# Multi-query attention on one core: every engine's order taken from a virtual-time plan, 231 units of the exponential on VectorE, the last product of each wholly on GpSimd

## The chip, the cores and the metric

The kernel runs on one core of a Trainium2 chip. The metric is device time in microseconds, the median of several runs. The engines are TensorE (PE in the profile; its weight loads are PEld), VectorE (DVE), ScalarE (ACT) and GpSimd (POOL). SyncE (SP) only issues transfers here. PSUM takes the matmul results; SBUF holds everything else.

## The reference, cut to what matters

Eight batches, 1,024 positions, 16 query heads of 64 columns, and one key and one value head per batch that all query heads share.

```python
def reference(q, k, v):              # q 8x1024x16x64, k and v 8x1024x64
    q = q.transpose(0, 2, 1, 3)
    scores = np.matmul(q, k.transpose(0, 1, 3, 2)) / np.sqrt(head_dim)
    weights = np.exp(scores - np.max(scores, axis=-1, keepdims=True))
    weights = weights / np.sum(weights, axis=-1, keepdims=True)
    return np.matmul(weights, v).transpose(0, 2, 1, 3)
```

## The kernel before

**Units.** The work is cut into 1,024 units (STEPS, numbered u). A unit belongs to a pair of heads p, to one half c of the 1,024 queries and to one block j of 128 keys; eight units (NKT) with the same p and c are a set. Two score matmuls (L261), one per head and each on half of the array's rows, write a 128x1024 tile of scores in PSUM. There are three such tiles (scp), so three units can be between their score matmuls and the reading of their scores. No maximum is subtracted; a check of the sums at the end (L377 on) sets a flag, and another path runs if it is bad.

**The exponential, two ways.** Most units go to ScalarE: one ACTIVATE (L274) makes a 128x1024 weight tile "wt". Every fifth unit from step 10 to step 1000, 200 in all, goes to VectorE (`vector_exp`, L210), in five steps:

- bits (L215): scores in PSUM to 16-bit integers in SBUF, a half-precision number whose exponent is roughly right;
- mantissa (L221) and power (L231): the fraction and the exponent cut out of these bits, SBUF to SBUF;
- square (L242): the mantissa times itself, SBUF to SBUF;
- product: bits times square. GpSimd makes columns 512 to 1023 (L243), VectorE columns 0 to 511 (L249). VE_U = 512 is the point of division.

Such a unit has three weight tiles: power, bits and product, which are multiplied by value tiles scaled by C0, 1 and C3. Its values therefore take three matmuls where a ScalarE unit takes one.

**Values.** For each set there are eight outputs (four blocks of 128 queries, two heads), numbered gg over the whole kernel. Each is a chain of 128x65 matmuls (L335) over the eight units' weight tiles, 8 plus 2 for every VectorE unit in the set; column 65 holds the sum. Seven outputs (GB) share one PSUM bank; there are two banks. When a bank is full, VectorE takes the reciprocal of its sums (`inverse`, L277) and multiplies (`finish`, L286) into an output tile "osb" of 56 groups, one of two, from which SP's queue stores 8 groups at a time (L314). The last set has its own loop (L365).

**What sets the order.** Each engine runs its instructions in the order in which the program issues them. That order is dealt out by hand. `step` (L402) issues the score matmuls and the exponential of one unit and then up to two of VectorE's waiting steps from the list `pend`. `plan` (L412) says after which units values are issued, and how many: DEAL = (1, 1, 0, 1, 0), so after three of each five units. TensorE therefore turns from values to scores and back three times in five units. Evictions enter `pend` ahead of the other steps. VectorE's half of the product is issued right after the bits of the next VectorE unit.

**The rest.** `after` (L434) prefetches the next batch: GpSimd issues the loads of q (L125) and of v (L108), SP the turning of q (L135), GpSimd scales the keys in two instructions (`prep_k`, L194) and VectorE scales the values (`prep_v`, L206). It is called for the units since the last values, behind those values.

Of the kernel before, what the change touches and what calls it, by code (L numbers as in the profile page):

```python
# [10 lines left out]
FP32 = mybir.dt.float32  # L11
# [13 lines left out]
DEAL = (1, 1, 0, 1, 0)  # L25
DEAL_AT = 1
VE_U = 512
VE_N = 1
VE_M = 5
# [3 lines left out]
def attention_main(ctx, tc, q, k, v, out, flag):  # L33
# [11 lines left out]
    nc = tc.nc  # L45
# [11 lines left out]
    OCH = 7  # L57
# [8 lines left out]
    wtp = ctx.enter_context(tc.tile_pool(name="wtp", bufs=24))  # L66
    w3p = ctx.enter_context(tc.tile_pool(name="w3p", bufs=6))
    mp = ctx.enter_context(tc.tile_pool(name="mp", bufs=2))
    osbp = ctx.enter_context(tc.tile_pool(name="osbp", bufs=2))
# [11 lines left out]

    kv = {}
# [4 lines left out]
    ot = {}  # L87
    pend = []
    product = []
    late = []  # L90
# [48 lines left out]
    def bank(name):  # L139
        return op.tile([P, 512], FP32, tag="ot", name=name)  # L140
# [69 lines left out]
    def vector_exp(sc, p, c, j):  # L210
        w3 = w3p.tile([P, 3, 2, QCH], FP16, tag="w3", name=f"we{p}_{c}_{j}")
        m = mp.tile([P, 2, QCH], FP16, tag="m", name=f"m{p}_{c}_{j}")
        m2 = mp.tile([P, 2, QCH], FP16, tag="m2", name=f"mm{p}_{c}_{j}")
        t = w3[:, 1].bitcast(I16)
        nc.vector.tensor_scalar(  # L215
            out=t, in0=sc, scalar1=15.0 * 1024, scalar2=0.0, op0=ALU.add, op1=ALU.max
        )
        if product:
            pend.append(product.pop())
        pend.append(  # L220
            lambda: nc.vector.tensor_scalar(  # L221
                out=m.bitcast(I16),
                in0=t,
                scalar1=0x3FF,
                scalar2=0x3C00,
                op0=ALU.bitwise_and,
                op1=ALU.bitwise_or,
            )
        )
        pend.append(  # L230
            lambda: nc.vector.tensor_scalar(  # L231
                out=w3[:, 0].bitcast(I16),
                in0=t,
                scalar1=0x7C00,
                scalar2=None,
                op0=ALU.bitwise_and,
            )
        )
        we, wu, mm = (x.rearrange("p h q -> p (h q)") for x in (w3[:, 1], w3[:, 2], m2))

        def square():
            nc.vector.tensor_tensor(out=m2, in0=m, in1=m, op=ALU.mult)  # L242
            nc.gpsimd.tensor_tensor(  # L243
                out=wu[:, VE_U:], in0=we[:, VE_U:], in1=mm[:, VE_U:], op=ALU.mult
            )

        pend.append(square)
        product.append(
            lambda: nc.vector.tensor_tensor(  # L249
                out=wu[:, :VE_U], in0=we[:, :VE_U], in1=mm[:, :VE_U], op=ALU.mult  # L250
            )
        )
        wt[(p, c, j)] = [(w3[:, 0], 1), (w3[:, 1], 0), (w3[:, 2], 2)]

    def scores(p, c, j, by_vector):
        b = p // HP
        sc = scp.tile([P, 2, QCH], FP32, tag="sc", name=f"sc{p}_{c}_{j}")
        k2t = kv[b]["k2t"]
        for hh in range(2):
            r = 64 * hh  # L260
            nc.tensor.matmul(  # L261
                sc[:, hh, :],
                k2t[r : r + 64, j * P : (j + 1) * P],
                qt[b][r : r + 64, p % HP, c * QCH : (c + 1) * QCH],
                start=True,
                stop=True,
                tile_position=(r, 0),
            )
        if by_vector:
            vector_exp(sc, p, c, j)  # L270
            return
        w = wtp.tile([P, 2, QCH], FP16, tag="wt", name=f"wt{p}_{c}_{j}")
        wt[(p, c, j)] = [(w, 0)]
        nc.scalar.activation(out=w, in_=sc, func=EXP, scale=escale, bias=math.log(CS))  # L274

    def inverse(o, g0, n):
        nc.vector.reciprocal(out=rec_all[:, g0 : g0 + n], in_=o[:, 0:n, D])  # L277

    def finish(o, g0, n):

        rec = rec_all[:, g0 : g0 + n]
        i0 = g0 % (OCH * GRP)
        if i0 == 0:
            osb[0] = osbp.tile([P, OCH * GRP, D], FP32, tag="osb", name=f"osb{g0}")
# [23 lines left out]
    def store(ob, g0, g1):  # L308
# [3 lines left out]
        j0 = g0 % (OCH * GRP)  # L312
# [8 lines left out]
    def values(gg):  # L321


        p, c = divmod(gg // GRP, NCH)
        g = gg % GRP
        qb, hh = divmod(g, 2)
        if gg % GB == 0:
            ot[0] = bank(f"ot{gg}")[:, 0 : GB * 72].rearrange("p (g f) -> p g f", f=72)
        o = ot[0]
        vp = kv[p // HP]["vp"]  # L330
        terms = [(j, w, i) for j in range(NKT) for w, i in wt[(p, c, j)]]

        def one(n, j, w, i):
            last = n == len(terms) - 1
            nc.tensor.matmul(  # L335
                o[:, gg % GB, 0 : D + 1],
                w[:, hh, qb * P : (qb + 1) * P],
                vp[:, i, j, 0 : D + 1],
                start=(n == 0),
                stop=last,  # L340
            )
            if not last:
                return
            if gg % GB == GB - 1 or gg == NG - GRP - 1:
                late.append((o, gg - gg % GB, gg % GB + 1))
            if g == GRP - 1:
                for x in range(NKT):
                    del wt[(p, c, x)]

        return [lambda n=n, t=t: one(n, *t) for n, t in enumerate(terms)]  # L350

    def last_values():
# [8 lines left out]
        for j in range(NKT):  # L361
            ((w, i),) = wt[(p, c, j)]
# [10 lines left out]
        for h in range(2):  # L373
            inverse(os[h], NG - GRP + 4 * h, 4)
            finish(os[h], NG - GRP + 4 * h, 4)
# [17 lines left out]
    LAG = 2 * NKT + 2  # L393
    STEPS = NP * NCH * NKT
    PSTEPS = NCH * NKT
    LAST_VE = max(u for u in range(STEPS - 2 * NKT + 1) if u * VE_N % VE_M < VE_N)
    HURRY = STEPS - NKT - 6

    def to_vector(u):
        return NKT <= u <= LAST_VE and u * VE_N % VE_M < VE_N  # L400

    def step(u):  # L402
        p, r = divmod(u, PSTEPS)
        c, j = divmod(r, NKT)
        scores(p, c, j, to_vector(u))
        for _ in range(2):
            if pend:
                pend.pop(0)()
        if product and u >= LAST_VE + 2 and not pend:
            product.pop()()  # L410

    def plan():  # L412

        upto = [0]
        for g in range(STEPS):
            many = sum(to_vector(g // GRP * NKT + j) for j in range(NKT))
            upto.append(upto[-1] + NKT + 2 * many)
        due = {}  # L420
        for u in range(STEPS):
            if u >= HURRY:
                if u % 2:
                    due[u] = None
                continue
            n, i = divmod(u - DEAL_AT, len(DEAL))
            if DEAL[i]:
                at = DEAL_AT + len(DEAL) * (n + sum(DEAL[: i + 1]) / sum(DEAL)) - LAG
                at = max(at, 0.0)
                g = int(at)  # L430
                due[u] = round(upto[g] + (at - g) * (upto[g + 1] - upto[g]))
        return due
# [28 lines left out]
    with tc.manual_schedule():  # L461
# [28 lines left out]
        nxt = made = 0  # L490
        todo = []
        due = plan()
        us = []
        for u in range(STEPS):
            step(u)
            us.append(u)
            if u not in due:
                continue
            new = []
            for f in late:  # L500
                new += [lambda f=f: inverse(*f), lambda f=f: finish(*f)]
            if len(new) == 2:
                new[1:1] = pend[:1]
                del pend[:1]
            pend[:0] = new
            del late[:]
            if due[u] is not None:
                while made < due[u]:
                    if not todo:
                        todo = values(nxt)  # L510
                        nxt += 1
                    todo.pop(0)()
                    made += 1
            else:
                for _ in range(4):
                    if not todo and nxt < STEPS - GRP and nxt // GRP * NKT + NKT + 3 <= u:
                        todo = values(nxt)
                        nxt += 1
                    for f in todo:
                        f()  # L520
                    todo = []
            for x in us:
                after(x)
            us = []
        assert nxt == STEPS - GRP
        assert not product
        for f in pend:
            f()
        for f in late:
            inverse(*f)  # L530
            finish(*f)
# [128 lines left out]
```

## Time and profile before

The median of three runs is 774.12 us (773.71 to 774.24). The profiled execution is one of its own.

| What | Value |
|---|---|
| Span of the profiled execution | 771.9 us |
| Granted TensorE clock, mean | 0.995 |
| ScalarE's first exponential starts, last ends | 7.26 us, 765.9 us |
| VectorE's first bits (L215), last bits | 15.18 us, 748.58 us |
| Last GpSimd product (L243) ends | 752.70 us |
| Matmuls of the last set (L365) start | 763.90 us |
| Mean of one mantissa / power / square | 428 / 434 / 692 ns |
| Mean of one half product on VectorE / on GpSimd | 437 / 1154 ns |
| Mean of one inverse / one finish | 195 / 622 ns |
| Key scaling on GpSimd (L194) | 14 of 1652 ns |
| q loads issued by GpSimd (L125) | 64 of 604 ns |

Busy time is given per engine and per line of the program. In a group line, the shapes are those of output and input, then the number of instructions, the busy time of all of them in us, the mean of one in ns, and behind the bar the time for which the engine stood idle just before them, with what ended it. In a timeline line, the start in us comes first, then the time taken, engine, line, operation and tiles. VectorE's successive instructions overlap a little at their ends, so the distance from start to start is shorter than the duration.

### The profile page before, as it was taken

To read this page: it belongs to the slowest core of one execution; us is meant where nothing else is said; L and a number is where in the kernel's file an instruction comes from. 1 tells how busy PE (TensorE), PEld (TensorE's weight loads), DVE (VectorE), ACT (ScalarE), POOL (GpSimd) and SP (SyncE) were. 2 spreads that over 40 slices of the span, in tenths; PEclk is the share of its full clock that TensorE was granted. 3 is DMA by queue.
4 is the path that set the end of the run, shared out by engine and by line. 5 is a ranking of instruction groups with operands and counts; after the bars stand their busy time and mean duration, and the time that the engine had idled before them with its cause. 6 is when DMAs were issued, how large, how long until landed. Compare 5 with 4: busy or idle time off the path is not lost.

```text
span 771.9 us, 31242 instructions
## 1 busy us (share of the span) xinstructions
PE 741.9 (96%) x13474; PEld 471.0 (61%) x13474; DVE 695.4 (90%) x1349; ACT 759.3 (98%) x827; POOL 298.5 (39%) x299
## 2 busy tenths in 40 slices
PE   5999999999999999999999999999999999999997
PEld 1566666666666666666666666666666666666665
DVE  3899989998999998999899999999999999899993
ACT  7999999999999999999999999999999999999996
POOL 4453334533344333454234532345333443332330
PEclk9899999999999999999999999999999999999999
DMA  9858436764265533775356764467535665212113
GB/s 185 125 102 125 98 70 100 96 131 98 59 117 111 111 71 84 105 125 96 85 99 96 101 120 95 83 105 110 104 78 84 105 124 98 57 43 57 43 44 85
DMA packets 168637, 73.87 MB, mean 96 GB/s; under 512 B 93744, under 2 KB 161328, under 8 KB 168496
## 3 DMA queue, kind: packets, MB, share of 16 engines
q1 hardware_dynamic: 148864, 53.76, 34.1%
q0 software_dynamic: 18576, 17.57, 17.1%
q8 instruction: 106, 1.74, 1.0%
q10 hardware_dynamic: 1056, 0.52, 0.3%
q14 instruction: 35, 0.29, 0.1%
HBM read 37.75 MB, written 33.55 MB: 92 GB/s over the span
## 4 chain that ended last, share of the span: by engine, by line
PE 41%; ACT 34%; issue 13%; DVE 10%; DMA 1%; ACTq 0%; DVEq 0%
ACT wt L274 34%; PE ot L335 22%; PE sc L261 19%; DVE we L215 3%; DVE mm L242 2%; DVE osb L286 1%; DVE we L249 1%; DVE m L221 1%; DMA qf<-in_q_dram 1%; DVE ge L381 0%; DVE rec_all L277 0%; DMA out_dram<-osb 0%; PE otl L365 0%; DVE vp L206 0%; DVE both L387 0%
## 5 line engine op out<-in xcount | busy, mean ns | idle before, releaser
L274 ACT ACTIVATE wt<-sc 128x1024 f16<-128x1024 f32 x824 | 756.8, 1084 | 2.6 <-PE sc L261 2.4
L335 PE MATMUL ot<-vp,wt 128*128 128x65 f16 x6528 | 430.1, 194 | 0.8 <-DVE osb L286 0.7
L335 PEld LDWEIGHTS <-wt 128*128 128x128 f16 x6528 | 328.1, 98 | 134.7 <-issue 134.6
L243 POOL TENSOR_TENSOR we<-we,mm 128x512 f16<-128x512 f16 x200 | 230.8, 1154 | 442.8 <-DVE mm L242 208.6
L261 PE MATMUL sc<-qt,k2t 64*128 64x512 f16 x2048 | 362.7, 386 | 18.8 <-ACT wt L274 13.8
L335 PE MATMUL ot<-vp,we 128*128 128x65 f16 x4800 | 351.6, 193 | 0.0
L215 DVE TENSOR_SCALAR we<-sc 128x1024 int16<-128x1024 f32 x200 | 244.2, 1221 | 48.0 <-PE sc L261 45.3
L335 PEld LDWEIGHTS <-we 128*128 128x128 f16 x4800 | 251.6, 97 | 43.9 <-issue 43.8
L261 PEld LDWEIGHTS <-k2t 64*128 64x128 f16 x2048 | 85.7, 94 | 109.7 <-issue 76.6
L242 DVE TENSOR_TENSOR mm<-m 128x1024 f16<-128x1024 f16 x200 | 138.3, 692 | 0.1
L286 DVE TENSOR_TENSOR osb<-ot,rec_all 128x448 f32<-128x448 f32 x146 | 90.7, 622 | 5.1 <-DMA out_dram<-osb 0.2
L249 DVE TENSOR_TENSOR we<-we,mm 128x512 f16<-128x512 f16 x200 | 87.3, 437 | 0.0
L231 DVE TENSOR_SCALAR we<-we 128x1024 int16<-128x1024 int16 x200 | 86.7, 434 | 0.0
L221 DVE TENSOR_SCALAR m<-we 128x1024 int16<-128x1024 int16 x200 | 85.5, 428 | 0.0
L125 POOL DMA_DIRECT2D q<-in_q_dram x64 | 38.4, 604 | 10.6 <-DMA qt<-q 8.3
L277 DVE RECIPROCAL rec_all<-ot 128x7 f32<-128x7 f32 x146 | 28.5, 195 | 7.3 <-PE ot L335 7.2
L194 POOL TENSOR_SCALAR k16d<-knat 128x512 f16<-128x512 f32 x14 | 23.0, 1652 | 0.1
L108 POOL DMA_DIRECT2D vp<-in_v_dram x8 | 7.6, 952 | 0.0
L206 DVE TENSOR_SCALAR vp<-vp 128x512 f16<-128x512 f16 x16 | 4.8, 343 | 1.0 <-DMA vp<-in_v_dram 1.0
L159 PE MATMUL kps<-ident,k 128*64 128x128 f16 x16 | 1.3, 314 | 4.4 <-DVE k L150 4.4
L188 DVE COPY qt<-qps 128x512 f16<-128x512 f16 (+1 forms) x2 | 1.1, 556 | 3.8 <-PE qps L175 3.8
L381 DVE TENSOR_SCALAR ge<-rec_all 128x128 f32<-128x128 f32 (+2 forms) x9 | 3.8, 421 | 0.0
(30 smaller groups left out, 21.9 us busy)
## 6 DMA issues: line engine op xcount, KB each, us to landing
out_dram<-osb SPq DMA_DIRECT2D x127, 256.0 KB, 2.6
q<-in_q_dram POOLq DMA_DIRECT2D x56, 256.0 KB, 4.4
knat<-in_k_dram SPq DMA_DIRECT2D x7, 256.0 KB, 3.3
q<-in_q_dram POOLq DMA_DIRECT2D x8, 192.0 KB, 7.5
vp<-in_v_dram POOLq DMA_DIRECT2D x8, 128.0 KB, 4.7
qt<-q SPq DMA_TRANSPOSE x64, 4.6
qf<-in_q_dram ACTq DMA_DIRECT2D x2, 256.0 KB, 4.4
knat<-in_k_dram SPq DMA_DIRECT2D x2, 128.0 KB, 3.8
```

Source lines behind the costliest of these rows:

```text
L125: nc.gpsimd.dma_start(out=q16[(b, c)], in_=q[b, c * P : (c + 1) * P, h0:, :].rearrange("p h d -> p (h d)"),)
L215: nc.vector.tensor_scalar(out=t, in0=sc, scalar1=15.0 * 1024, scalar2=0.0, op0=ALU.add, op1=ALU.max)
L221: lambda: nc.vector.tensor_scalar(out=m.bitcast(I16), in0=t, scalar1=0x3FF, scalar2=0x3C00, op0=ALU.bitwise_and, op1=ALU.bitwise_or,)
L231: lambda: nc.vector.tensor_scalar(out=w3[:, 0].bitcast(I16), in0=t, scalar1=0x7C00, scalar2=None, op0=ALU.bitwise_and,)
L242: nc.vector.tensor_tensor(out=m2, in0=m, in1=m, op=ALU.mult)
L243: nc.gpsimd.tensor_tensor(out=wu[:, VE_U:], in0=we[:, VE_U:], in1=mm[:, VE_U:], op=ALU.mult)
L249: lambda: nc.vector.tensor_tensor(out=wu[:, :VE_U], in0=we[:, :VE_U], in1=mm[:, :VE_U], op=ALU.mult)
L261: nc.tensor.matmul(sc[:, hh, :], k2t[r : r + 64, j * P : (j + 1) * P], qt[b][r : r + 64, p % HP, c * QCH : (c + 1) * QCH], start=True, sto ...
L274: nc.scalar.activation(out=w, in_=sc, func=EXP, scale=escale, bias=math.log(CS))
L277: nc.vector.reciprocal(out=rec_all[:, g0 : g0 + n], in_=o[:, 0:n, D])
L286: nc.vector.tensor_tensor(out=ob[:, i0 : i0 + n, :], in0=o[:, 0:n, 0:D], in1=rec.unsqueeze(2).broadcast_to([P, n, D]), op=ALU.mult,)
L335: nc.tensor.matmul(o[:, gg % GB, 0 : D + 1], w[:, hh, qb * P : (qb + 1) * P], vp[:, i, j, 0 : D + 1], start=(n == 0), stop=last,)
```

## The change

The constants DEAL, VE_U, VE_N and VE_M go; planned costs and limits in ns come in. The step function, the lists `pend`, `product` and `late`, and the two-way deal go too. `plan` now keeps a clock for each of TensorE, VectorE, ScalarE and GpSimd and the times at which every buffer comes free, and writes down one list of operations, sorted by planned start. The program issues them in that order. What each operation computes is as before except for the product: it is one GpSimd instruction of 1,024 columns in place of two halves on two engines.

A unit may go to VectorE (`to_v`) only if two or more score tiles are free and it is the first to be issued in its turn, if the unit before it did not, if the planned backlog allows it, and if fewer than 0.23 of the units since the eighth have gone; the last 12 units do not. The planned choice of VectorE's next step takes what can start soonest (bits up to 150 ns early), and among equals follows ORDER. A turn of TensorE to scores is taken when two score tiles are free, or one where ScalarE would otherwise run out. The order of the values' terms within an output changes: first one tile of each unit, then the powers, then the products. Value matmuls are planned one by one, each when its weights have been ready for SAFE = 1000 ns. Buffers: 20 "wt" tiles for 24, 8 three-part tiles for 6, and three output tiles of 28 groups for two of 56; a store ends at the next multiple of 8 groups or at the end of its output tile, so there are 18 more stores.

```diff
-DEAL = (1, 1, 0, 1, 0)
-VE_U = 512
-VE_N = 1
-VE_M = 5
+N_WT = 20
+N_W3 = 8
+N_M = 2
+T_PAIR = 214.0
+T_IN = 96.0
+T_OUT = 106.0
+T_MM = 30.5
+T_SCORE = 480.0
+T_ACT = 917.0
+ACT_DONE = 1110.0
+MM_DONE = 270.0
+T_CUBE = 2190.0
+VE_TAIL = 115.0
+GP_TAIL = 100.0
+VE_COST = {"bits": 1140.0, "mantissa": 335.0, "power": 335.0,
+           "square": 604.0, "inverse": 210.0, "finish": 541.0}
+ORDER = {"bits": 0, "finish": 1, "inverse": 2, "square": 3, "mantissa": 4, "power": 5}
+AHEAD = 150.0
+VE_SLACK = 900.0
+GP_SLACK = 6000.0
+V_END = 12
+RATE = 0.23
+NEAR = 2000.0
+WAIT = 0.0
+SAFE = 1000.0
...
-            nc.gpsimd.tensor_tensor(
-                out=wu[:, VE_U:], in0=we[:, VE_U:], in1=mm[:, VE_U:], op=ALU.mult
-            )
...
-            lambda: nc.vector.tensor_tensor(
-                out=wu[:, :VE_U], in0=we[:, :VE_U], in1=mm[:, :VE_U], op=ALU.mult
-            )
+    def ve_cube(u):
+        w3 = ve[u]["w3"]
+        nc.gpsimd.tensor_tensor(
+            out=w3[:, 2], in0=w3[:, 1], in1=ve[u].pop("m2"), op=ALU.mult
+        )
...
-            e += GRP // 2 if e >= NG - GRP else GRP
+            e = min(e + (GRP // 2 if e >= NG - GRP else GRP - e % GRP), e - e % OGR + OGR)
...
+    def terms_of(h):
+        us = range(h * NKT, (h + 1) * NKT)
+        own = [(u, 0) for u in us]
+        return own + [(u, i) for i in (1, 2) for u in us if kinds[u] == "V"]
...
+        def vector_step(limit):
...
+                s = max(t_ve, r)
+                if what == "mantissa":
+                    s = max(s, min(m_used["m"]))
+                if what == "square":
+                    s = max(s, min(m_used["m2"]))
+                if what == "bits":
+                    s = max(s, min(w3_used))
+                key = (max(s - t_ve - (AHEAD if what == "bits" else 0), 0), ORDER[what], v)
...
+            else:
+                m_used["m"][live.pop(("m", v))] = done
+                i, _ = hold(m_used["m2"], s)
+                gs = max(t_gp, done)
+                emit(gs, "cube", v)
+                t_gp = gs + T_CUBE
+                m_used["m2"][i] = t_gp
+                ready[v, 2] = t_gp + VE_TAIL + GP_TAIL
...
+        def issue(t, first):
...
+            to_v = (
+                first
+                and NKT <= u < STEPS - V_END
+                and max(t_ve, s) + backlog() < s + T_SCORE + VE_SLACK
+                and max(t_gp, s) < s + GP_SLACK
+                and kinds.get(u - 1) != "V"
+                and made_v < (u - NKT + 1) * RATE
+                and min(w3_used) < s
+            )
...
+            n_free = sum(f <= t_pe for f in free)
+            go = n_free > 1
+            if n_free == 1:
+                other = sorted(late_free(i) for i in range(3))[1]
+                go = max(other, t_pe) + T_IN + T_SCORE > t_act + WAIT and t_pe + NEAR >= t_act - T_IN - T_SCORE
+            if u < STEPS and go:
+                t = t_pe + (T_IN if mode == "v" else 0)
+                k = 0
+                while u < STEPS and k < n_free and issue(t, n_free > 1 and k == 0):
+                    t += T_PAIR
+                    k += 1
...
+                r = ready.get(x, float("inf"))
+                if r < float("inf"):
+                    r += SAFE
+                if n == 0 and gg % GB == 0:
+                    r = max(r, bank_free[gg // GB % 2])
+                if r <= t_pe:
+                    s = t_pe + (T_OUT if mode == "s" else 0)
+                    mode = "v"
+                    emit(s, "value", gg, n)
+                    t_pe = s + T_MM
...
+        return [(what, args) for _, _, what, args in sorted(ops, key=lambda x: x[:2])]
...
-        for u in range(STEPS):
-            step(u)
...
+        for what, args in plan():
+            run[what](*args)
         last_values()
```

More of the change, by code (lines that the diff above doesn't have):

```diff
@@ L24 @@
 CS = 2.1471603163479376
-DEAL = (1, 1, 0, 1, 0)
-DEAL_AT = 1
-VE_U = 512
-VE_N = 1
-VE_M = 5
+N_WT = 20
[12 more added lines that the diff above has]
+GP_TAIL = 100.0
+VE_COST = {
+    "bits": 1140.0,
+    "mantissa": 335.0,
+    "power": 335.0,
+    "square": 604.0,
+    "inverse": 210.0,
+    "finish": 541.0,
+}
+ORDER = {"bits": 0, "finish": 1, "inverse": 2, "square": 3, "mantissa": 4, "power": 5}
[6 more added lines that the diff above has]
+WAIT = 0.0
+T_BITS = 1255.0
+SAFE = 1000.0
 @with_exitstack
@@ L80, in attention_main @@
     qf = consts.tile([P, NKT, P], FP32, name="qf")
+    sc = {}
+    ve = {}
+    ots = {}
     kv = {}
@@ L208, in prep_v, with scores @@
             )
[L210 to L216, printed above, removed]
-        )
[L218 to L227, printed above, removed]
-            )
[L229 to L243, printed above, removed]
-                out=wu[:, VE_U:], in0=we[:, VE_U:], in1=mm[:, VE_U:], op=ALU.mult
[L245 to L249, printed above, removed]
-                out=wu[:, :VE_U], in0=we[:, :VE_U], in1=mm[:, :VE_U], op=ALU.mult
[L251 to L255, printed above, removed]
+    def scores(u):
+        p, c, j = where(u)
         b = p // HP
-        sc = scp.tile([P, 2, QCH], FP32, tag="sc", name=f"sc{p}_{c}_{j}")
+        sc[u] = scp.tile([P, 2, QCH], FP32, tag="sc", name=f"sc{p}_{c}_{j}")
         k2t = kv[b]["k2t"]
@@ L268, in scores, with scalar_exp, ve_bits @@
             )
-        if by_vector:
-            vector_exp(sc, p, c, j)
-            return
+    def scalar_exp(u):
+        p, c, j = where(u)
         w = wtp.tile([P, 2, QCH], FP16, tag="wt", name=f"wt{p}_{c}_{j}")
-        wt[(p, c, j)] = [(w, 0)]
-        nc.scalar.activation(out=w, in_=sc, func=EXP, scale=escale, bias=math.log(CS))
-    def inverse(o, g0, n):
+        wt[u] = [(w, 0)]
+        nc.scalar.activation(out=w, in_=sc.pop(u), func=EXP, scale=escale, bias=math.log(CS))
+    def ve_bits(u):
+        p, c, j = where(u)
+        w3 = w3p.tile([P, 3, 2, QCH], FP16, tag="w3", name=f"we{p}_{c}_{j}")
+        wt[u] = [(w3[:, 1], 0), (w3[:, 0], 1), (w3[:, 2], 2)]
+        ve[u] = {"w3": w3}
+        nc.vector.tensor_scalar(
+            out=w3[:, 1].bitcast(I16),
+            in0=sc.pop(u),
+            scalar1=15.0 * 1024,
+            scalar2=0.0,
+            op0=ALU.add,
+            op1=ALU.max,
+        )
@@ new lines, in ve_mantissa, with ve_power @@
+    def ve_mantissa(u):
+        ve[u]["m"] = mp.tile([P, 2, QCH], FP16, tag="m", name=f"m{u}")
+        nc.vector.tensor_scalar(
+            out=ve[u]["m"].bitcast(I16),
+            in0=ve[u]["w3"][:, 1].bitcast(I16),
+            scalar1=0x3FF,
+            scalar2=0x3C00,
+            op0=ALU.bitwise_and,
+            op1=ALU.bitwise_or,
+        )
+    def ve_power(u):
+        nc.vector.tensor_scalar(
+            out=ve[u]["w3"][:, 0].bitcast(I16),
+            in0=ve[u]["w3"][:, 1].bitcast(I16),
+            scalar1=0x7C00,
+            scalar2=None,
+            op0=ALU.bitwise_and,
+        )
@@ L277, in inverse, with ve_square, finish @@
+    def ve_square(u):
+        ve[u]["m2"] = mp.tile([P, 2, QCH], FP16, tag="m2", name=f"mm{u}")
+        m = ve[u].pop("m")
+        nc.vector.tensor_tensor(out=ve[u]["m2"], in0=m, in1=m, op=ALU.mult)
+    def ve_cube(u):
+        w3 = ve[u]["w3"]
+        nc.gpsimd.tensor_tensor(
+            out=w3[:, 2], in0=w3[:, 1], in1=ve[u].pop("m2"), op=ALU.mult
+        )
+    def inverse(g0, n):
+        o = ots[g0]
         nc.vector.reciprocal(out=rec_all[:, g0 : g0 + n], in_=o[:, 0:n, D])
-    def finish(o, g0, n):
+    def finish(g0, n):
+        o = ots.pop(g0)
@@ L319, in store, with value @@
         )
-    def values(gg):
-        p, c = divmod(gg // GRP, NCH)
-        g = gg % GRP
+    def value(gg, n):
+        h, g = divmod(gg, GRP)
         qb, hh = divmod(g, 2)
[L327 to L350, printed above, removed]
+        g0 = bank_of(gg)[0]
+        if g0 not in ots:
+            ots[g0] = bank(f"ot{g0}")[:, 0 : GB * 72].rearrange("p (g f) -> p g f", f=72)
+        terms = terms_of(h)
+        u, i = terms[n]
+        w, ci = wt[u][i]
+        nc.tensor.matmul(
+            ots[g0][:, gg - g0, 0 : D + 1],
+            w[:, hh, qb * P : (qb + 1) * P],
+            kv[h // (HP * NCH)]["vp"][:, ci, u % NKT, 0 : D + 1],
+            start=(n == 0),
+            stop=(n == len(terms) - 1),
+        )
+        if g == GRP - 1 and n == len(terms) - 1:
+            for j in range(NKT):
+                del wt[h * NKT + j]
     def last_values():
@@ L412, in plan, with where @@
-    def plan():
[L416 to L420, printed above, removed]
-        for u in range(STEPS):
[L422 to L432, printed above, removed]
+    def where(u):
+        p, r = divmod(u, PSTEPS)
+        return (p, *divmod(r, NKT))
@@ L489, in attention_main @@
             turn_q(0, c)
[L490 to L494, printed above, removed]
-            step(u)
[L496 to L531, printed above, removed]
+        run = {
+            "score": scores,
+            "act": scalar_exp,
+            "bits": ve_bits,
+            "mantissa": ve_mantissa,
+            "power": ve_power,
+            "square": ve_square,
+            "cube": ve_cube,
+            "value": value,
+            "inverse": inverse,
+            "finish": finish,
+            "after": after,
+        }
+        for what, args in plan():
+            run[what](*args)
         last_values()
```

195 lines of the change are left out of this document (166 added, 29 removed).

## The prediction

> **What bounds the kernel now.** I read the page's busy shares and groups first, then the chain of waits, then the timeline of VectorE and GpSimd alone, round single products.
>
> ```profile
> span 771.9 us, 31242 instructions
> PE 741.9 (96%) x13474; PEld 471.0 (61%) x13474; DVE 695.4 (90%) x1349; ACT 759.3 (98%) x827; POOL 298.5 (39%) x299
> PE 41%; ACT 34%; issue 13%; DVE 10%; DMA 1%; ACTq 0%; DVEq 0%
> L274 ACT ACTIVATE wt<-sc 128x1024 f16<-128x1024 f32 x824 | 756.8, 1084 | 2.6 <-PE sc L261 2.4
> L243 POOL TENSOR_TENSOR we<-we,mm 128x512 f16<-128x512 f16 x200 | 230.8, 1154 | 442.8 <-DVE mm L242 208.6
> L215 DVE TENSOR_SCALAR we<-sc 128x1024 int16<-128x1024 f32 x200 | 244.2, 1221 | 48.0 <-PE sc L261 45.3
> L242 DVE TENSOR_TENSOR mm<-m 128x1024 f16<-128x1024 f16 x200 | 138.3, 692 | 0.1
> ```
>
> ScalarE has 2.6 us of idle time between its first and last exponential: it sets the pace, 756.8 / 824 = 0.918 us a unit. The chain names TensorE more often, but TensorE has room. From successive starts between 50 and 740 us, value matmuls follow each other every 0.0305 us, a pair of score matmuls takes 0.214, and each turn from values to scores and back costs 0.20 (0.126 and 0.318 in place of 0.030 and 0.214). The whole kernel has 11,328 values, 1,024 pairs and 614 turns: 345.5 + 219.1 + 122.8 = 687 us; the rest of its 742 busy is waiting inside the pipeline.
>
> The timeline decides this case. First VectorE at two places, then GpSimd at the same two:
>
> ```profile
> 121.34 0.68 DVE L242 TENSOR_TENSOR mm<-m 128x1024 f16<-128x1024 f16 x1
> 121.94 0.20 DVE L277 RECIPROCAL rec_all<-ot 128x7 f32<-128x7 f32 x1
> 122.18 0.62 DVE L286 TENSOR_TENSOR osb<-ot,rec_all 128x448 f32<-128x448 f32 x1
> 122.72 0.69 DVE L381 TENSOR_SCALAR ge<-rec_all 128x128 f32<-128x128 f32 x1
> ...
> 751.56 0.62 DVE L286 TENSOR_TENSOR osb<-ot,rec_all 128x448 f32<-128x448 f32 x1
> 752.10 0.89 DVE L249 TENSOR_TENSOR we<-we,mm 128x512 f16<-128x512 f16 x1
> ```
> ```profile
> 122.17 1.16 POOL L243 TENSOR_TENSOR we<-we,mm 128x512 f16<-128x512 f16 x1 [1.73 <-DVE rec_all L277]
> ...
> 751.55 1.15 POOL L243 TENSOR_TENSOR we<-we,mm 128x512 f16<-128x512 f16 x1 [1.96 <-DVE rec_all L277]
> ```
>
> L249 usually takes 0.41 us. Here it takes 0.89 and ends 0.29 after GpSimd's product does (752.99 against 752.70). L381 takes 0.21 when alone; here 0.69, ending 0.08 after the product. In 200 products no SBUF-to-SBUF instruction of VectorE both started and finished inside L243. What reads PSUM is untouched: L286 takes 0.62 beside a product and without one, L215 1.21 alone and 1.22 beside one. So **a GpSimd product and a VectorE instruction that works from SBUF to SBUF exclude each other**, while L215, L277 and L286 may run under it. Before, the half product (1.15) almost fits under L215 (1.14 from start to start), so the exclusion costs little. The next rows show a GpSimd instruction of another kind giving way in its middle, VectorE first:
>
> ```profile
> 53.79 0.79 DVE L249 TENSOR_TENSOR we<-we,mm 128x512 f16<-128x512 f16 x1
> 54.50 0.41 DVE L221 TENSOR_SCALAR m<-we 128x1024 int16<-128x1024 int16 x1
> 54.84 0.82 DVE L231 TENSOR_SCALAR we<-we 128x1024 int16<-128x1024 int16 x1
> 55.58 1.08 DVE L242 TENSOR_TENSOR mm<-m 128x1024 f16<-128x1024 f16 x1
> ```
> ```profile
> 53.70 3.30 POOL L194 TENSOR_SCALAR k16d<-knat 128x512 f16<-128x512 f32 x2
> ```
>
> L249 and L221 end inside the first key scaling; L231 waits for its end.
>
> **The change, part by part.** *ScalarE* loses 31 units: 31 x 0.918 = 28.5 us. If it still set the end, the span would be 743.4.
>
> *TensorE* gains 31 x 16 = 496 values, 15.1 us. Its turns lie between 512 (always two units a turn) and about 627 (one single turn for each VectorE unit), 102 to 125 us. Sum 360.6 + 219.1 + 102 to 125 = 682 to 705, under 743 in either case.
>
> *VectorE* loses L249, 200 x 0.332 = 66 us, and gains 31 units of 1.14 + 0.335 + 0.335 + 0.604 = 2.414 (start to start), 75 us. With 146 evictions of 0.23 + 0.54 and some 12 us of checks and copies it holds 231 x 2.414 + 112 + 12 = 682 us, 92% of 743: enough, if nothing holds it up.
>
> *GpSimd* gets 231 products of 1,024 columns. No row shows one: it lies between 1.15 (if width were free) and 2.31 (twice 1.154). The smallest GpSimd instructions, its 128x1 memsets, take 0.10, so I take 2 x 1.154 - 0.10 = 2.21, near the double since the work is twice the work. With the key scaling (23 us), q loads (38) and v loads (8): 511 + 69 = 580 us, no bound of its own.
>
> *The exclusion* is what the edit pays for. The plan's costs have no term for it. At ScalarE's new pace a VectorE unit must come every 728 / 231 = 3.15 us. One unit's mantissa, power and square run from SBUF to SBUF (1.274 us) and its product takes 2.21: 3.48 of 3.15 us. Before it was 1.274 + 0.332 + 1.154 = 2.76 of 3.69 ((748.58 - 15.18) / 199 between L215 starts). L215 and the evictions (1.14 + 0.49 a unit) fit under the product, but they are shorter than it. Step by step: the product ends at 0; the next unit's mantissa, held up, ends at 0.28 (L249's row, also 0.41 alone), so it counts as started at -0.14; power starts at 0.20, square at 0.53 and ends at 1.21; GpSimd starts 0.14 later (the median between L242's end and L243's start) and ends at 3.57. Each unit costs **3.566 us**, as the next L215 has been done meanwhile.
>
> Two costs have bounds on both sides. GpSimd may give way in its middle, as in the key scaling, and hide the 0.14 and the hand-overs: 3.2 us a unit, down by 0.37 x 230 = 85. Against that, the plan ranks "finish" above "square", "mantissa" and "power", so an eviction can fall between mantissa and square, where no product covers it: up to 146 x (0.69 x 0.54 + 0.22 x 0.23) = 61 us (the shares of finishes and inverses that get ready when mantissa, power or, for a finish, the bits before them are next, if that is spread evenly over a unit's 3.1 us). They point opposite ways, and I take neither.
>
> The key scalings stand between two products on GpSimd: 3.30 us where 1.35 is free, 7 x 1.95 = 14 us. The q loads (0.60 each) fit into the 1.35.
>
> Where the stall goes: a late product holds up the third term's value matmuls; queued behind these on TensorE are the next scores, and ScalarE waits for those. Its slack of 865 - 728 us takes it up. The other edits cost nothing, each behind a named cover: 18 more stores on SP (landing in 2.6 us; L286 waited 0.2 us for one in the whole run), with three output tiles of 28 groups for two of 56; the per-unit loads that move ahead of the values; and rings of 20 and 8 tiles for 24 and 6, with nothing before waiting on either. Without that cover a missing tile costs one 0.9 us exponential.
>
> **The sum.** First square ends at 16.4 (17.8 in the trace, two units earlier at most); 230 x 3.566 = 820.2; the last product, 0.14 + 2.21, to 838.9; key scalings 13.7, to 852.6; then 3.5 us of values and the last 8.0 (763.9 to 771.9 in the trace): span 864.1. The profiled span of 771.9 stands 2.2 below the median of 774.12, so 866.3.
>
> The Trainium skill, page "SBUF — State Buffer", section "Who interferes with whom", calls this an exclusive lock between the two engines, held for the whole instruction. L243's rows agree (0.29 and 0.08 behind its end); L194's rows do not, as two instructions finished inside. By the rule the sum stays 866; by L194's rows it is the packed case below.
>
> **Rivals.** *Packed:* the exclusion holds but the turns interlock, at 3.2 us a unit: 16.4 + 736 + 2.4 + 13.7 + 11.5 + 2.2 = 782. L194's rows speak for it; against it, L243 has not given way once between 0.55 us after its start and its end, and each square must still be done before its own product.
>
> *Cover (faster):* the wide product holds VectorE for much less of its length than the narrow one, and ScalarE sets the end: 743.4 + 2.2 = 746, up to 757 if TensorE, at 95%, misses some turns. It decides where 1.274 + 0.14 + the time held is under 3.15, that is under 1.73 of the product's 2.21 us. For it: nothing shows the first 0.55 us of a product. Against: that alone leaves 1.66 held, just below the point, and only if it is all free.
>
> *Displaced evictions:* the 61 us in full and nothing packed: 927. For it the ranking; against it, evictions that get ready during a square still go under the product.
>
> That the units aren't 231 is no rival: the made_v rule with 0.23 of 1,005 units gives it.
>
> **How the numbers follow.** Serial exclusion 0.55, packed 0.25, cover 0.14, displaced 0.06. The forecast is 866. Serial runs from 835 (part packed) to 910 (half displaced). The range takes in the packed case and most of the way to the displaced one, 776 to 920, and leaves out cover and the far end. About 0.2% is what a measurement of this kernel can tell from no change: faster 0.14, same 0.02 (packed a shade tighter), slower 0.84.
>
> **What would show it.** Right: mantissa's mean well over 1 us in place of 0.43, with each ending some 0.28 after a product; GpSimd's product at 2.2 us, 231 times; L274's successor at 84% of the span with long waits for scores. Wrong: mantissa and power at 0.42 while products run, ScalarE at 98%, a span near 743; or a product well below 2.2 us, which shortens each cycle by as much.

## The result and the profile after

The changed kernel takes 966.37 us (963.49 to 967.87), the kernel before 774.18 in the same comparison: a ratio of 1.2477 (95% interval 1.2457 to 1.2497). The forecast was 866, with a range of 776 to 920. The direction was right, the size was not, and the time lies outside the range.

The page after, its busy shares, its chain by engine and the groups that answer to those shown before. The new lines are L256 for ScalarE's exponential, L299 for the product, L263 for bits, L274 for mantissa, L284 for power, L295 for square and L243 for the scores:

```profile
span 965.8 us, 32208 instructions
PE 791.2 (82%) x13970; PEld 514.6 (53%) x13970; DVE 905.3 (94%) x1273; ACT 765.9 (79%) x796; POOL 565.0 (58%) x330
DVE 63%; PE 18%; issue 17%; DMA 1%; ACT 1%; DVEq 0%; SPq 0%; ACTq 0%
L256 ACT ACTIVATE wt<-sc 128x1024 f16<-128x1024 f32 x793 | 763.4, 1024 | 189.4 <-PE sc L243 182.7
L299 POOL TENSOR_TENSOR we<-we,mm 128x1024 f16<-128x1024 f16 x231 | 497.8, 2155 | 375.6 <-DVE mm L295 173.4
L243 PE MATMUL sc<-qt,k2t 64*128 64x512 f16 x2048 | 355.4, 404 | 157.2 <-DVE we L263 151.8
L263 DVE TENSOR_SCALAR we<-sc 128x1024 int16<-128x1024 f32 x231 | 280.0, 1212 | 27.4 <-PE sc L243 27.1
L284 DVE TENSOR_SCALAR we<-we 128x1024 int16<-128x1024 int16 x231 | 206.0, 892 | 0.0
L295 DVE TENSOR_TENSOR mm<-m 128x1024 f16<-128x1024 f16 x231 | 180.6, 782 | 0.0
L274 DVE TENSOR_SCALAR m<-we 128x1024 int16<-128x1024 int16 x231 | 173.1, 749 | 3.9
```

The mantissa and power of before, for comparison:

```profile
L231 DVE TENSOR_SCALAR we<-we 128x1024 int16<-128x1024 int16 x200 | 86.7, 434 | 0.0
L221 DVE TENSOR_SCALAR m<-we 128x1024 int16<-128x1024 int16 x200 | 85.5, 428 | 0.0
```

ScalarE, which had been idle for 2.6 us, is now idle for 189, nearly all of it behind scores. TensorE's scores wait 151.8 us for bits to free a score tile. VectorE, at the head of the queue, counts as busy for 94% and leads the chain. But its work hardly grew (682 us by the forecast's sum, 200 x (2.414 + 0.332) + 124 = 673 before at the same costs): its instructions got longer. The mantissa went from 428 to 749 ns, the power from 434 to 892, the square from 692 to 782, while L263, which reads PSUM, stayed at 1212. That a busy engine may be standing still shows when the mean of the same shape is compared in two profiles.

The timeline shows what the time is made of, VectorE first, then GpSimd over the same stretch:

```profile
509.12 1.22 DVE L263 TENSOR_SCALAR we<-sc 128x1024 int16<-128x1024 f32 x1
510.25 0.68 DVE L295 TENSOR_TENSOR mm<-m 128x1024 f16<-128x1024 f16 x1
510.85 0.42 DVE L274 TENSOR_SCALAR m<-we 128x1024 int16<-128x1024 int16 x1
511.19 2.35 DVE L284 TENSOR_SCALAR we<-we 128x1024 int16<-128x1024 int16 x1
513.46 0.19 DVE L305 RECIPROCAL rec_all<-ot 128x7 f32<-128x7 f32 x1
513.57 0.63 DVE L295 TENSOR_TENSOR mm<-m 128x1024 f16<-128x1024 f16 x1
514.13 0.61 DVE L314 TENSOR_TENSOR osb<-ot,rec_all 128x448 f32<-128x448 f32 x1
514.66 1.21 DVE L263 TENSOR_SCALAR we<-sc 128x1024 int16<-128x1024 f32 x1
```
```profile
511.02 2.23 POOL L299 TENSOR_TENSOR we<-we,mm 128x1024 f16<-128x1024 f16 x1 [3.42 <-DVE mm L295]
514.35 2.12 POOL L299 TENSOR_TENSOR we<-we,mm 128x1024 f16<-128x1024 f16 x1 [1.10 <-PE sc L243]
```

The bits of the next unit (509.12) were issued ahead of the square of this one (510.25). So what follows the square here is no cover but the next mantissa and power. The mantissa slips in before the product starts; the power (511.19) stands through the rest of it and ends at 513.54, 0.29 after the product (513.25). The bits at 514.66 do lie under the second product.

Counted over the trace from starts and ends, 76 of 231 squares were issued with the next unit's bits already done (none of 200 before). 90 products had no bits under them. The mantissas, powers and squares that started inside these took 1.57 us per product more than their usual 0.42, 0.42 and 0.68. 132 products had bits under them for over 0.8 us, and cost 0.46 each by the same count; 9 lie between. In all, mantissas, powers and squares exceed their usual lengths by 212 us (before: 7 us). The distance from square to square is 4.04 us, where the forecast had 3.566.

### The profile page after: what moved, and what is told of

The parts are those of the page before. It is cut to its first block, busy times and chain, and to the rows that moved or that the text cites. A ratio compares the mean times of both kernels' runs of the same rounds, so it can differ in the third digit from the quotient of the medians.

```text
span 965.8 us, 32208 instructions
## 1 busy us (share of the span) xinstructions
PE 791.2 (82%) x13970; PEld 514.6 (53%) x13970; DVE 905.3 (94%) x1273; ACT 765.9 (79%) x796; POOL 565.0 (58%) x330
## 4 chain that ended last, share of the span: by engine, by line
DVE 63%; PE 18%; issue 17%; DMA 1%; ACT 1%; DVEq 0%; SPq 0%; ACTq 0%
DVE we L263 22%; DVE mm L295 14%; DVE m L274 12%; PE ot L358 10%; PE sc L243 8%; DVE osb L314 6%; DVE we L284 5%; DVE rec_all L305 2%; DVE ge L399 1%; ACT wt L256 1%; DVE vp L232 0%; DMA qf<-in_q_dram 0%; DMA out_dram<-osb 0%; DMA qt<-q 0%; DVE both L405 0%
## 5 line engine op out<-in xcount | busy, mean ns | idle before, releaser
L256 ACT ACTIVATE wt<-sc 128x1024 f16<-128x1024 f32 x793 | 763.4, 1024 | 189.4 <-PE sc L243 182.7
L299 POOL TENSOR_TENSOR we<-we,mm 128x1024 f16<-128x1024 f16 x231 | 497.8, 2155 | 375.6 <-DVE mm L295 173.4
L243 PE MATMUL sc<-qt,k2t 64*128 64x512 f16 x2048 | 355.4, 404 | 157.2 <-DVE we L263 151.8
L358 PE MATMUL ot<-vp,we 128*128 128x65 f16 x5544 | 454.1, 198 | 7.2 <-DVE we L284 6.5
L358 PE MATMUL ot<-vp,wt 128*128 128x65 f16 x6280 | 451.8, 199 | 0.0
L358 PEld LDWEIGHTS <-wt 128*128 128x128 f16 x6280 | 338.6, 101 | 122.0 <-issue 122.0
L358 PEld LDWEIGHTS <-we 128*128 128x128 f16 x5544 | 338.2, 100 | 119.3 <-issue 102.3
L263 DVE TENSOR_SCALAR we<-sc 128x1024 int16<-128x1024 f32 x231 | 280.0, 1212 | 27.4 <-PE sc L243 27.1
L284 DVE TENSOR_SCALAR we<-we 128x1024 int16<-128x1024 int16 x231 | 206.0, 892 | 0.0
L243 PEld LDWEIGHTS <-k2t 64*128 64x128 f16 x2048 | 83.8, 94 | 197.5 <-issue 159.8
L295 DVE TENSOR_TENSOR mm<-m 128x1024 f16<-128x1024 f16 x231 | 180.6, 782 | 0.0
L274 DVE TENSOR_SCALAR m<-we 128x1024 int16<-128x1024 int16 x231 | 173.1, 749 | 3.9
```

What stands on the lines that cost most here:

```text
L243: nc.tensor.matmul(sc[u][:, hh, :], k2t[r : r + 64, j * P : (j + 1) * P], qt[b][r : r + 64, p % HP, c * QCH : (c + 1) * QCH], start=True, ...
L256: nc.scalar.activation(out=w, in_=sc.pop(u), func=EXP, scale=escale, bias=math.log(CS))
L263: nc.vector.tensor_scalar(out=w3[:, 1].bitcast(I16), in0=sc.pop(u), scalar1=15.0 * 1024, scalar2=0.0, op0=ALU.add, op1=ALU.max,)
L274: nc.vector.tensor_scalar(out=ve[u]["m"].bitcast(I16), in0=ve[u]["w3"][:, 1].bitcast(I16), scalar1=0x3FF, scalar2=0x3C00, op0=ALU.bitwise_and,
L284: nc.vector.tensor_scalar(out=ve[u]["w3"][:, 0].bitcast(I16), in0=ve[u]["w3"][:, 1].bitcast(I16), scalar1=0x7C00, scalar2=None, op0=ALU.bi ...
L295: nc.vector.tensor_tensor(out=ve[u]["m2"], in0=m, in1=m, op=ALU.mult)
```

## The experiments

In what follows "stall" is that sum over mantissas, powers and squares, and "period" the mean distance from one square to the next.

**e1, e2: the changed order with a shorter product.** The order of every engine stays; only the width of GpSimd's instruction changes, and with it which columns the third term's values read.

```diff
-            out=w3[:, 2], in0=w3[:, 1], in1=ve[u].pop("m2"), op=ALU.mult
+            out=w3[:, 2, 1, 384:], in0=w3[:, 1, 1, 384:], in1=ve[u].pop("m2")[:, 1, 384:], op=ALU.mult
...
-            w[:, hh, qb * P : (qb + 1) * P],
+            w[:, 1, 384:] if ci == 2 else w[:, hh, qb * P : (qb + 1) * P],
```

That is e1; e2 has `[:, 2, 1]`, `[:, 1, 1]` and `[:, 1]` in the first line, and `1 if ci == 2 else hh` in the second.

> Every order of the changed kernel is kept, but GpSimd makes 128 of the product's 1,024 columns, and the third term's values read those 128 columns each time (seven eighths of the product are left out). Theory (exclusion: VectorE stands still while a wide product runs): a product of about 0.36 us in place of 2.16 leaves almost no stall; the 214 us by which VectorE's mantissas, powers and squares are longer than their usual 0.42, 0.42 and 0.68 fall below 20, and the time is 745 to 775 us. Rival (the new static order by itself starves the engines): nothing of the order changes, so 940 to 970. Rival (the clock: the granted clock of 0.94 makes TensorE the bound): the matmuls are the same, so the time stays over 900 and the clock at 0.94.

> The same with 512 of the 1,024 columns on GpSimd, the third term's values reading head 1's half for both heads (half the product is left out). Theory: a product of about 1.10 to 1.15 us; the 90 products without L263 under them lose about 1.05 us of stall each, the 132 with it lose most of their 0.46: 214 - 95 - 50 = some 70 us of stall left, 800 to 840 us. If GpSimd's occupation rather than the exclusion were the cause, the time would go with GpSimd's busy time, 231 x 1.05 = 243 us less, down to the bound of ScalarE near 745.

e1 took 774.68 us (ratio 1.0008, 0.9996 to 1.002), at the upper edge of its range, e2 818.69 (1.0576, 1.0529 to 1.0624), inside its own. Here is e1's and then e2's listing by line, the product and the two steps behind it:

```profile
L256 ACT ACTIVATE wt<-sc 128x1024 f16<-128x1024 f32 x793 | 746.2, 1032 | 11.9 <-PE sc L243 5.1
L284 DVE TENSOR_SCALAR we<-we 128x1024 int16<-128x1024 int16 x231 | 109.4, 473 | 0.0
L299 POOL TENSOR_TENSOR we<-we,mm 128x128 f16<-128x128 f16 x231 | 106.3, 460 | 564.4 <-DVE mm L295 256.6 <-PE sc L243 167.0 <-DVE rec_all L305 93.4
L274 DVE TENSOR_SCALAR m<-we 128x1024 int16<-128x1024 int16 x231 | 97.8, 423 | 3.9
```
```profile
L256 ACT ACTIVATE wt<-sc 128x1024 f16<-128x1024 f32 x793 | 755.1, 1027 | 45.4 <-PE sc L243 37.4
L299 POOL TENSOR_TENSOR we<-we,mm 128x512 f16<-128x512 f16 x231 | 274.4, 1188 | 445.5 <-DVE mm L295 196.3 <-PE sc L243 143.1 <-DVE rec_all L305 82.9
L284 DVE TENSOR_SCALAR we<-we 128x1024 int16<-128x1024 int16 x231 | 147.6, 639 | 0.0
L274 DVE TENSOR_SCALAR m<-we 128x1024 int16<-128x1024 int16 x231 | 107.1, 464 | 3.9
```

With the same list of instructions on every engine, a product of 0.46, 1.19 and 2.16 us gives a stall of 16, 71 and 212 us and a time of 775, 819 and 966. All 192 us of the loss hang on the product's length. That the static order starves the engines by itself falls. So does the clock as a cause of its own: e1's matmuls are those of the changed kernel, and its granted clock is 0.998 against 0.94. Whether a long product costs by holding VectorE or merely by keeping GpSimd occupied, e8 decides below.

e1 says one more thing. With almost no exclusion left, the change still gains nothing on 774: TensorE is busy for 96% of e1, VectorE for 92%, and ScalarE waits a little at many places: its exponentials start 0.955 us apart on average, for 0.920 before, which over 793 of them is 28 of the 29 us between 746 and 775.

**e3, e5: the same product in another order.** e5 adds the first pair of lines to the plan's choice for VectorE, so that bits stay behind an earlier unit's steps; e3 adds the second pair as well, so that evictions do too.

```diff
+                if what == "bits" and any(y[0] != "bits" and y[1] < v for y in todo):
+                    continue
                 s = max(t_ve, r)
...
             for k, (r, what, g0, nn) in enumerate(evict):
+                if any(y[0] != "bits" for y in todo):
+                    continue
                 s = max(t_ve, r)
```

> Whole product on GpSimd, 231 units; the plan may not put a unit's bits ahead of an earlier unit's square (76 of 231 are), evictions as they fall. Theory: every product then has L263 under it and a unit costs 3.51 us; in about 100 units the finish still falls between mantissa and square, where nothing covers it, 100 x 0.54 = 54 us: 16.4 + 230 x 3.51 + 54 + 2.3 + 14 + 11.5 + 2.2 = 908, 885 to 930 us. Rival (where the bits stand doesn't matter, the stall is one of the product's length alone): 955 to 970.

> The whole product on GpSimd, 231 units, but the plan may not put a unit's bits ahead of an earlier unit's square, nor an eviction between bits and square, so that bits and evictions all fall under a product. Theory: the cycle of the prediction with the measured product, 1.21 + 0.14 + 2.16 = 3.51 us: 16.4 + 230 x 3.51 + 2.3 + 14 + 11.5 + 2.2 = 854 us, 840 to 875; period between squares 3.5 to 3.6 in place of 4.04. Rival (what costs is the wide product as such, wherever it stands): 950 to 970. Rival (VectorE simply has too much work, 231 units): no gain either, since its work is the same.

e5 took 917.89 us (1.1854, 1.183 to 1.1878), as expected; e3 took 927.48 (1.1982, 1.1958 to 1.2006), 52 us above its range. The product was 2.15 and 2.12 us, as wide as ever, and the work the same: to put the bits behind the square is worth 48 us, so the order counts. But in e3 the stall fell to 135 us, below e5's 177, and the time did not follow. Its timeline shows the unit that the forecast had worked out, VectorE and then GpSimd:

```profile
305.40 0.67 DVE L295 TENSOR_TENSOR mm<-m 128x1024 f16<-128x1024 f16 x1
306.00 0.19 DVE L305 RECIPROCAL rec_all<-ot 128x7 f32<-128x7 f32 x1
306.22 0.62 DVE L314 TENSOR_TENSOR osb<-ot,rec_all 128x448 f32<-128x448 f32 x1
306.77 1.21 DVE L263 TENSOR_SCALAR we<-sc 128x1024 int16<-128x1024 f32 x1
308.01 0.62 DVE L274 TENSOR_SCALAR m<-we 128x1024 int16<-128x1024 int16 x1
308.56 0.41 DVE L284 TENSOR_SCALAR we<-we 128x1024 int16<-128x1024 int16 x1
308.89 0.68 DVE L295 TENSOR_TENSOR mm<-m 128x1024 f16<-128x1024 f16 x1
```
```profile
306.23 2.12 POOL L299 TENSOR_TENSOR we<-we,mm 128x1024 f16<-128x1024 f16 x1 [0.98 <-DVE rec_all L305]
```

From square to square: 308.89 - 305.40 = 3.49 us, the expected 3.51. Of e3's 230 distances, the 126 with no eviction and no checks or copies in them have a mean of 3.59, 0.10 of it idle. The rest do not: one eviction, 60 times, 3.84 (0.41 idle); two, 29 times, 4.17, since two evictions and the bits (0.77 + 0.77 + 1.14) are longer than a product; and once 12.0, 7.3 of it idle. Over 3.51 all 230 come to 83 us. The expectation had allowed 14 of these, for key scalings; the other 69 are most of the 73 by which e3 missed 854. Holding the evictions back for the cover bunches them, and TensorE then waits for a PSUM bank, which it did not in e5:

```profile
PE ot L358 <- DVE osb L314: 57.8, 38, 7.9
```

(From e3's list of waits: who waited for whom, us in total, times, the longest.) A cover bought with a later eviction is paid for at the bank.

**e4: the old order with the wide product.** VectorE's half goes, GpSimd does all 1,024 columns for the 200 units.

```diff
-            nc.gpsimd.tensor_tensor(
-                out=wu[:, VE_U:], in0=we[:, VE_U:], in1=mm[:, VE_U:], op=ALU.mult
-            )
+            nc.gpsimd.tensor_tensor(out=wu, in0=we, in1=mm, op=ALU.mult)
...
-        product.append(
-            lambda: nc.vector.tensor_tensor(
-                out=wu[:, :VE_U], in0=we[:, :VE_U], in1=mm[:, :VE_U], op=ALU.mult
-            )
-        )
```

> The kernel before with its 200 units and its order, its product wholly on GpSimd and VectorE's half of it gone. Theory: its order puts the next bits and the evictions behind each square, and its period is 3.69 us, above the 3.51 that the exclusion asks for: 773 to 790 us, ScalarE still close to 98%. Rival (the wide product is what costs): 200 x (2.16 - 1.15) = 200 us more less VectorE's 66, about 900.

792.45 us (1.023, 1.0213 to 1.0247), 2 us above the range and far from 900. GpSimd's 200 products took 2127 ns each. The same wide product that goes with 192 us in the new order costs 18 net in the old one, where VectorE is rid of its half of the product, bits and evictions stand behind each square, and a unit had 3.69 us to itself; the period is now 3.78 and the stall 66 us. Since 200 units are fewer than 231, e4 does not separate the order from the number; e5, at 231 units, does so for the bits.

**e9: the old order with the new number.** VE_N, VE_M = 3, 13 give 231 units, with the product in halves as before.

> The kernel before with VE_N, VE_M = 3, 13 in place of 1, 5: 228 or so units on VectorE in the old order, products halved as they were. It asks what the number of units does by itself. ScalarE would need 26 us less, but VectorE needs 228 x 2.746 + 124 = 750 us and TensorE some 700: theory (three engines are near their bound, so the number gains nothing): 772 to 800 us. Rival (ScalarE sets the end and the number alone is worth 26 us): 748 to 755.

815.08 us (1.053, 1.0512 to 1.0547), beyond the range on the slow side. The stall is 11 us, so this is not the exclusion: VectorE is at 96% and has 78% of the chain. The number alone is worth 41 us of loss, not 26 of gain. At 231 units VectorE has no room for its half of the product, and in every order tried here that gave this half to GpSimd as well, the exclusion took more than was saved.

**e6, e7: the plan told of the exclusion.** Mantissa, power, square (and product) may not start before GpSimd's clock; bits wait for an earlier unit's square; an eviction may not stand between bits and square unless a product is running.

```diff
+                if what == "bits" and any(y[0] in ("mantissa", "power", "square") and y[1] < v for y in todo):
+                    continue
...
+                if what != "bits":
+                    s = max(s, t_gp)
...
+                if t_gp <= t_ve and any(y[0] in ("mantissa", "power", "square") for y in todo):
+                    continue
...
-RATE = 0.23
+RATE = 0.205
```

That is e6. e7 has RATE 0.215, T_CUBE 1130, a backlog limit VE_SLACK of 1500 in place of 900, and VectorE's half of the product as a sixth step of cost 332.

> Whole product on GpSimd, and the plan told of the exclusion: mantissa, power and square may not start before GpSimd's clock, bits not ahead of an earlier unit's square, evictions between bits and square only where no product is running to cover them; 206 units (RATE 0.205). Theory: a unit has 767 / 206 = 3.7 us, more than the 3.51 it needs, as in the kernel before with a wide product (792 us): 780 to 805 us. Rival (a static list from a plan can't hold on the chip): over 850.

> The same plan with the product halved again: 512 columns on GpSimd, planned at 1.13 us, and 512 on VectorE, planned at 0.332 behind it; 216 units (RATE 0.215). Theory: a unit needs 1.21 + 0.14 + 1.15 + 0.33 = 2.83 us under the exclusion and VectorE 216 x 2.746 + 124 = 717 us, so ScalarE with 808 units (742 us) and TensorE (11,648 values, about 700 us) set the end: 765 to 790 us, where the version at 128 columns, without any exclusion to speak of, took 775. Under 772 would beat the kernel before. Rival (a static list can't hold on the chip): over 830.

e6 took 816.66 us (1.0549, 1.0532 to 1.0567), 12 above its range; e7 786.04 (1.0154, 1.0137 to 1.0171), inside it. So a static list does hold: e6 keeps the whole product on GpSimd and is 150 us faster than the changed kernel, with 25 units fewer; how the 150 divide between the order and the number is not shown. In e7 the stall is gone (10 us) and three engines stand near their bound, TensorE at 95%, VectorE at 93%, ScalarE at 97%. None of the versions tried beats the kernel before.

**e8: a GpSimd instruction with one input.** The packed case rested on the key scaling, inside which VectorE's instructions had finished. e8 puts an instruction of that kind in the product's place.

```diff
-        nc.gpsimd.tensor_tensor(
-            out=w3[:, 2], in0=w3[:, 1], in1=ve[u].pop("m2"), op=ALU.mult
+        nc.gpsimd.tensor_scalar(
+            out=w3[:, 2], in0=ve[u].pop("m2"), scalar1=1.0, scalar2=None, op0=ALU.mult
```

> The changed kernel's order, but GpSimd's instruction reads one tile instead of two: it copies the square times 1.0 into the third term (the product is left out). It is of the kind of the key scaling, L194 before, inside which two of VectorE's instructions finished. Theory of the prediction's packed case (such an instruction gives way in its middle): some of VectorE's mantissas, powers and squares start and finish inside it, none did inside the product, and the stall per us of GpSimd's instruction is below the product's 214 us for 498. Rival (every GpSimd instruction holds VectorE to its end): none finishes inside, each that started inside ends 0.28 us or more behind it. Length of the instruction 1.1 to 3.3 us (one or two times L194's 1.62, or as short as the half product); time 850 to 1000 us.

884.65 us (1.1427, 1.1404 to 1.145), inside its range: GpSimd's instruction is longer (2831 ns for 2155), GpSimd is busy for 81% in place of 58%, and yet the kernel is 82 us faster and its stall 137 us for 212. So neither the length of GpSimd's instruction nor its occupation sets the loss by itself; what counts is whether VectorE is held meanwhile. VectorE, then GpSimd:

```profile
301.19 1.01 DVE L274 TENSOR_SCALAR m<-we 128x1024 int16<-128x1024 int16 x1
302.12 0.41 DVE L284 TENSOR_SCALAR we<-we 128x1024 int16<-128x1024 int16 x1
302.46 0.68 DVE L295 TENSOR_TENSOR mm<-m 128x1024 f16<-128x1024 f16 x1
```
```profile
300.88 5.50 POOL L299 TENSOR_SCALAR we<-mm 128x1024 f16<-128x1024 f16 x2 [2.23 <-DVE mm L295]
```

All three finish inside the first of the two, which ends at 303.65. Over the trace, 378 of 475 mantissas, powers and squares that started inside such an instruction also finished inside it. In the changed kernel, 203 started inside a product and not one finished there; the least by which one ended behind it is 0.28 us. In these runs only the one-input form gives way, so the packed case was not open to this change.

## Why the prediction was wrong, point by point

**Right.** GpSimd's product and VectorE's SBUF-to-SBUF instructions exclude each other, and this sets the end (e1, e2, e8). The product's length: 2.21 forecast, 2.155 measured. The end of a held instruction, 0.28 us behind. The cycle of a covered unit: 3.566, or 3.51 with the measured product, and 3.49 in the unit shown of e3, with a mean of 3.59 over its 126 plain ones. The signs named for it: mantissa's 749 ns fell short of "well over 1 us", because the power took the larger share, 892 where it was to have the usual 0.43; GpSimd's 2.16 us 231 times came; ScalarE's share was 79% for 84%.

**The step that failed** is the cost of a unit: "Each unit costs **3.566 us**, as the next L215 has been done meanwhile." The next unit's bits had not been under the product in 90 of 231 cases. The plan ranks bits first, and VectorE was 92% full by the forecast's own sum. In 75 of the 90 cases bits had come ahead of an earlier unit's square, and left behind it, apart from evictions, only instructions that the product stops. Measured 4.04, 230 times: 929.5 us in place of 820.2 and 13.7 for the key scalings, which fall inside it. That is 96 of the 102 us by which the span was missed (965.8 against 864.1); the start (first square ends at 19.6, not 16.4) and the tail (14.4 us for 11.5) have 3 each. e5 undoes this step alone and gets 48 us back.

The trace of the changed kernel shows what the 96 us are made of. Between the first square and the last, VectorE stalled for 212 us and was idle for 37, of which 26 lie just before bits, nearly all of it spent waiting for scores. The 681 us left are the work that the forecast had at 682, so its account of the work held. Its cycle and key scalings had left 820.2 + 13.7 - 682 = 152 us for the stall and nothing for idling. So about 60 us are stall beyond the forecast's, and 37 are idle time that it had put at nothing.

**The path to ScalarE** was another than forecast, too. There a late product was to hold up value matmuls and the scores queued behind them. In the trace value matmuls and their weight loads waited 9 us for products; the scores waited 151.8 us for bits to free a score tile.

**Its neighbour**, the displaced evictions, was taken at nothing, against a gain from packing. The gain does not exist (e8), so nothing stood against the loss. e5's remaining 177 - 135 = 42 us of stall over e3, where evictions are covered, is not far from the 54 that its expectation gave them; but e3's time shows that covering them by holding them back doesn't pay. That the 42 us are the evictions' is not shown. How the loss beyond e5's 48 us divides between evictions, idle time and the lower clock is not settled.

**Cover**, the rival on the faster side, is refuted twice: a power that started 0.10 us after a product's start was held to its end, and even a product of 0.46 us left 775, not 746. The sum behind that number took TensorE's 682 to 705 us as covered by 743; e1, with TensorE busy for 96% and VectorE for 92%, shows that it was not; which of the two costs ScalarE those 28 us is not shown.

## What to carry to other kernels

Where two engines exclude each other, count per unit what each must run alone, and then read the order for what stands under the long instruction: the cover has to be there in each round, not on average. A planner that ranks work by readiness can move just this cover away, and its own account (each step at its unhindered cost) doesn't show it. Before work is moved to an idle engine, look in the trace for instructions of others that end a fixed time behind that engine's own; they give the price.

## What the runs showed of the hardware

A two-input product on GpSimd holds the mantissas, powers and squares of VectorE that start inside it until it ends: 203 times of 203 in the changed kernel, the earliest 0.10 us after the product's start, and 872 of 872 over the five kernels with the whole product (e3, e4, e5, e6 and the changed one). A one-input instruction of the same width takes longer (2.76 us at the least against 2.11) and lets 378 of 475 through. And the granted clock fell where TensorE had to wait, with the same number of matmuls: 0.998 in e1, 0.992 in e2, 0.971 in e5, 0.952 in e3 and 0.94 in the changed kernel. Its record in the trace knows two values, full and half: half for 5 us in e1, 57 in e5, 92 in e3 and 118 in the changed kernel. TensorE's busy share doesn't give the clock by itself, as it is 85% in both e3 and e5.
